# Two branch products as seven quarter products, gates through tanh, and places and order from tables in a hybrid decoder layer

## The chip, the cores and the metric

The kernel runs on one core of one Trainium2 chip. The metric is the device time of one execution in microseconds (us). Before the change it is 788.07 us, the median of three runs (787.36 to 788.13). Engines are called PE (TensorE, matrix products), ACT (ScalarE), DVE (VectorE), POOL (GpSimd) and SP (SyncE, which here issues transfers only); each runs its own instruction list in order and waits for the others by semaphores. POOL's list holds both its own arithmetic and the transfers that it issues.

## The reference

One decoder layer on a sequence of 512 tokens of width 1024, in float32. Three attention branches stand side by side: a sliding-window branch with sinks and bias (SWA), a stick-breaking branch (SB) and a cross attention to 256 memory tokens (MEM). Each has its own output product and a sigmoid gate; then come the output product, and a SwiGLU FFN of width 2816.

```python
u = rms_norm(h, ln_mix_pre[l])
proj = jnp.einsum('bsd,de->bse', u, w_in[l])
qa, ka, va, qb, kb, vb, qm, gl = jnp.split(proj, split_idx, axis=-1)
...
g = jax.nn.sigmoid(gl.reshape(B, S, N_BRANCH, D))
merged = (g[:, :, 0] * jnp.einsum('bse,ed->bsd', y_swa, w_branch_swa[l])
          + g[:, :, 1] * jnp.einsum('bse,ed->bsd', y_sb, w_branch_sb[l])
          + g[:, :, 2] * jnp.einsum('bse,ed->bsd', y_mem, w_branch_mem[l]))
mix = jnp.einsum('bsd,de->bse', merged, w_out[l])
h = h + rms_norm(mix, ln_mix_post[l])
...
ffn = jnp.einsum('bsf,fd->bsd', a, w_down[l])
h = h + rms_norm(ffn, ln_ffn_post[l])
```

Each branch output `y` is 512 x 512 and its product is 512 x 512 by 512 x 1024. The gate logits `gl` are 512 x 1024 by 1024 x 1024 for each branch.

## The kernel before, in words

**Products in three.** Every float32 operand is cut into a high part `hi` in a reduced format (an ACT copy, line 137) and the rest `lo` (a DVE subtraction, line 138). A product is the sum of three matmuls, hi x hi (line 169), hi x lo (170) and lo x hi (171). Nearly all have a left tile of 128 x 128 and 512 or 256 columns at the right.

**The stream of weights.** All products up to the gates run through one object, `Stream dn`. It is a list of units; a unit is one weight tile of up to 128 x 1024 that is loaded (tile `raw`, four buffers), split by ACT and DVE into `hi` and `lo` (four buffers each), and used by a generator of matmuls. Loads run four units ahead of the matmuls and splits three. The attention code calls `dn.run(us)` between its steps, which puts about so many microseconds of the stream's matmuls behind the step, so that PE has work while softmaxes and scans run on the other engines.

**Order of the stream.** Keys and queries of SB, values, keys of SWA, queries of SWA between the memory's keys and values, queries of MEM; then the branch product of SB, the gate of SB, the gate and the branch product of SWA, the gate and the branch product of MEM. Behind it come the transposes of the merged branches (`merge`) and the output product (`mx`).

**Gates as seven quarter products.** A gate product is cut into quarters of both operands and done as seven quarter products in place of eight (`QUART`, in the order p1, p2, p5, p3, p6, p7, p4), each in two weight units of 12 matmuls. The sums of weight quarters that this needs are made by transfers: `q_issue` adds a quarter from memory into a `raw` tile that is already there, on POOL's queue (line 446), six units ahead of its use. The sums of token quarters are made the same way from a second copy of the input, `xq` (lines 455 to 495), scaled on ACT. What a quarter product leaves in PSUM is kept by an ACT copy (line 540) or joined by DVE in `q_end`; p5 and p3 gather in one PSUM bank, and p1, p6, p7 and p4 in another.

**Branch products.** `branch_t` does a branch in the plain way: four token tiles, two column halves, four k steps. Its weight tiles come two a half, so a branch is four weight units. For SWA and MEM, DVE multiplies the PSUM result by the gate (line 599), and POOL adds what was there (line 602).

**Gates and tables of ACT.** `gated` applies Sigmoid on ACT. The softmaxes need Exp and the stick-breaking Ln and Exp, which lie in another table set than Sigmoid, so ACT loads tables several times (line 202 and others).

**What sets the order.** Each engine's list is in the order in which the program writes the instructions, with a scheduler and some explicit dependencies (`after`, `high_priority`, `later`) where it matters. PSUM is two pools, one of six banks (`aps`) and one of two (`dps`).

Of the kernel before, what the change touches and what calls it, by code (L numbers as in the profile page):

```python
# [17 lines left out]
P = 128  # L18
# [11 lines left out]
QM_FIRST = 3  # L30
WARM = 10

# [74 lines left out]
def tile_kernel(ctx, tc, a):  # L107
    nc = tc.nc
# [4 lines left out]
    psd = ctx.enter_context(tc.tile_pool(name="psd", bufs=2, space=bass.MemoryType.PSUM))  # L113
    psa = ctx.enter_context(tc.tile_pool(name="psa", bufs=6, space=bass.MemoryType.PSUM))
    drm = ctx.enter_context(tc.tile_pool(name="drm", bufs=1, space=bass.MemoryType.DRAM))

    first = ExitStack()
    wp = first.enter_context(tc.tile_pool(name="wp", bufs=4))
    cst = first.enter_context(tc.tile_pool(name="cst", bufs=1))

    def ck(name, dt=F32):
        return ckp.tile([P, 512], dt, tag="ck", name=name)

    def small(name, n=4):
        return sm.tile([P, 8], F32, tag="s", name=name)[:, :n]

    def dps(name):
        return psd.tile([P, 512], F32, tag="d", name=name)

    def aps(name):  # L130
        return psa.tile([P, 512], F32, tag="a", name=name)
# [14 lines left out]
    def w_load(src, n):  # L146
        uid[0] += 1
        raw = wp.tile([P, 1024], F32, tag="raw", name=f"raw{uid[0]}")
        nc.sync.dma_start(raw[:, :n], src)
        return raw  # L150

    def w_split(raw, n):
        uid[0] += 1
        hi = wp.tile([P, 1024], F32R, tag="hi", name=f"hi{uid[0]}", bufs=4)
        lo = wp.tile([P, 1024], F32R, tag="lo", name=f"lo{uid[0]}", bufs=4)
# [32 lines left out]
    def after(ins, first):  # L188
        dep = mybir.DependencyInfo(mybir.DependencyClass.NoSync, mybir.DependencyReason.DATA)
        tc.add_manual_dep(ins.ins, first.ins.name, dep, reason="order")  # L190

# [17 lines left out]
    def const(name, shape, pool=cst):  # L209
        t = pool.tile(shape, F32, name=f"c_{name}")  # L210
        nc.sync.dma_start(t[:, :], a[name])
        return t
# [3 lines left out]
    ones = cst.tile([P, P], F32, name="ones")  # L216
# [11 lines left out]
    def rstd_of(name, acc, n, bank):  # L228
# [6 lines left out]
        rb = cst.tile([P, n], F32, name=f"rb_{name}")  # L235
# [5 lines left out]
        rs = cst.tile([P, n // P], F32, name=f"rs_{name}")  # L241
# [46 lines left out]
    def proj(kind, idx):  # L288
        def gen(hi, lo):
            begun = first_ps.get((kind, idx))  # L290
            ps = begun or (aps if kind == "kb" or (kind, idx) == ("qb", 2) else dps)(f"{kind}{idx}")
# [6 lines left out]
            def evac():  # L298
                with tc.high_priority():
                    nc.vector.scalar_tensor_tensor(t[:, :], ps[:, :], s, st["rb"][:, :], op0=ALU.mult, op1=ALU.mult)  # L300
# [14 lines left out]

    def sigmoids(b):

        st.setdefault("sigmoid", set()).add(b)
        for f in st.pop(f"raw{b}", ()):
            f()  # L320

    def val(h, q):
        def gen(hi, lo):
            if q == 0:
                st["pv"] = [aps(f"pv{h}{t}") for t in range(NT)]
            for i in range(3 if q < 2 else 2):
                k = 3 * q + i
                for t in range(NT):
# [3 lines left out]
                    if k == KC - 1:  # L332
                        with tc.high_priority():
# [4 lines left out]
                                None,  # L338
                                op0=ALU.mult,
                            )  # L340
# [3 lines left out]
    v_all = cst.tile([P, NT * 640], F32, name="v_all")  # L344
# [32 lines left out]
    def mem_split():  # L377
# [13 lines left out]
        dn.later(5.0, lambda: st.update(zip(("mrs", "mrb"), rstd_of("m", acc, M, dps))))  # L391

    def mem_keys(i):
        def gen(hi, lo):
# [7 lines left out]
            with tc.high_priority():  # L402
                nc.vector.tensor_tensor(t, ps[:, :M], st["mrb"][:, :], op=ALU.mult)
# [5 lines left out]
    def mem_vals(q):  # L409
        def gen(hi, lo):  # L410
            if q == 0:
                st["pmv"] = [aps(f"pmv{t}") for t in range(2)]
            for i in range(2):
                k = 2 * q + i
                for t in range(2):
# [3 lines left out]
                    if k == KC - 1:  # L419
                        vt = ck(f"mv{t}")  # L420
                        with tc.high_priority():
                            nc.vector.tensor_scalar(
                                vt[:, :], st["pmv"][t][:, :], st["mrs"][:, t : t + 1], None, op0=ALU.mult
# [8 lines left out]
    QBANK = dict(p1="x", p6="x", p7="x", p4="x", p5="y", p3="y", p2="w")  # L432
# [4 lines left out]
    def q_issue(b, p, c):  # L437
# [8 lines left out]
        nc.gpsimd.dma_start(t[:, :], src, accum_op=ALU.add)  # L446
# [9 lines left out]
    def x_quarters(j, i):  # L456
        for c in range(2):
            t = quarter[(j, i, c)] = ck(f"xq{j}{i}{c}")
            nc.sync.dma_start(t[:, :], a["xq"][:, i, 4 * j + 2 * c : 4 * j + 2 * c + 2].rearrange("p k n -> p (k n)"))

    def x_gained(out, x, j, c, g):
        for k in range(2):
            sl, kk = slice(k * 256, (k + 1) * 256), 4 * j + 2 * c + k
            nc.scalar.activation(out[:, sl], x[:, sl], AF.Identity, scale=g[:, kk : kk + 1])

    def q_sum1(c):

        x_gained(quarter[(1, 1, c)], quarter[(1, 1, c)], 1, c, g_neg)
        x_gained(quarter[(0, 1, c)], quarter[(0, 1, c)], 0, c, g_pre)
        nc.gpsimd.dma_start(quarter[(1, 1, c)][:, :], quarter[(0, 1, c)][:, :], accum_op=ALU.add)  # L470
        quarter[("p5", c)] = quarter.pop((1, 1, c))

    def q_sum2():

        for c in range(2):
            t = quarter[("p6", c)] = ck(f"xq6{c}")
            x_gained(t, quarter[(0, 0, c)], 0, c, g_neg)
            nc.gpsimd.dma_start(t[:, :], quarter[("p5", c)][:, :], accum_op=ALU.add)

    def q_gain(j):  # L480
        for c in range(2):
            x_gained(quarter[(j, 0, c)], quarter[(j, 0, c)], j, c, g_pre)

    def q_sum3():

        for c in range(2):
            t = quarter[("p3", c)] = quarter.pop((1, 0, c))
            nc.gpsimd.dma_start(t[:, :], quarter[("p6", c)][:, :], accum_op=ALU.add)

    def q_sum4():  # L490

        for c in range(2):
            x = quarter.pop((0, 1, c))
            nc.scalar.mul(x[:, :], x[:, :], -1.0)
            t = quarter[("p7", c)] = quarter.pop((0, 0, c))
            nc.gpsimd.dma_start(t[:, :], x[:, :], accum_op=ALU.add)
# [21 lines left out]
    def gated(b, t, h, x):  # L518

        fn(x[:, :], x[:, :], AF.Sigmoid, scale=st["rs"][:, t : t + 1])  # L520
        if b == SB:
            acc = acc_t[(t, h)]
            nc.vector.tensor_tensor(acc[:, :], acc[:, :], x[:, :], op=ALU.mult)
        else:
            gate_t[(b, t, h)] = x

    def gate_there(b, t, h, x):
        if b != SB:
            gate_t[(b, t, h)] = x
        if b in st.get("sigmoid", ()):  # L530
            dn.later(2.0, lambda: gated(b, t, h, x))
        else:
            st.setdefault(f"raw{b}", []).append(lambda: gated(b, t, h, x))

    def q_end(b, p, i):
        ps = qbank[(QBANK[p], i)]
        if p in ("p1", "p5", "p6", "p7"):
            t = qkeep[(p, i)] = ck(f"gq{b}{p}{i}")

            st["chain"] = nc.scalar.copy(t[:, :], ps[:, :])  # L540
        if p == "p2":
            t = qkeep.pop(("p1", i))
            nc.vector.tensor_tensor(t[:, :], ps[:, :], t[:, :], op=ALU.add)
            gate_there(b, i, 0, t)
        elif p == "p6":
            t = qkeep.pop(("p6", i))
            nc.vector.tensor_tensor(t[:, :], qbank[("y", i)][:, :], t[:, :], op=ALU.subtract)
            gate_there(b, i, 1, t)
        elif p == "p7":
            t, x = qkeep.pop(("p5", i)), qkeep.pop(("p7", i))  # L550
            nc.vector.tensor_tensor(t[:, :], t[:, :], x[:, :], op=ALU.subtract)
            gate_there(b, 2 + i, 1, t)
        elif p == "p4":
            t = ck(f"gq{b}{p}{i}")
            fn(t[:, :], ps[:, :], AF.Sigmoid, scale=st["rs"][:, 2 + i : 3 + i])
            if b == SB:
                acc = acc_t[(2 + i, 0)]
                nc.vector.tensor_tensor(acc[:, :], acc[:, :], t[:, :], op=ALU.mult)
            else:
                gate_t[(b, 2 + i, 0)] = t  # L560

    def quart(b, p, c):
        def gen(hi, lo):
            for i in range(2):
                key = (QBANK[p], i)
                first = p in ("p1", "p5", "p2") and c == 0
                if first:
                    qbank[key] = (dps if p == "p2" else aps)(f"g{b}{p}{i}")
                for k in range(2):
                    mm3_behind(qbank[key][:, :], q_left(p, c, k, i), cols((hi, lo), k * 512, 512), first and k == 0, c == 1 and k == 1)  # L570
                yield 1.36
                if c == 1:
                    q_end(b, p, i)
# [3 lines left out]
    def branch_t(b, h, q):  # L577


        def gen(hi, lo):  # L580
# [3 lines left out]
            for t in range(NT):  # L584
# [7 lines left out]
                if b == SB:  # L592
                    acc_t[(t, h)] = ck(f"bs{t}{h}")
                    with tc.high_priority():
                        nc.vector.tensor_copy(acc_t[(t, h)][:, :], ps[:, :])
                    continue
                g = gate_t[(b, t, h)]
                with tc.high_priority():
                    nc.vector.tensor_tensor(g[:, :], ps[:, :], g[:, :], op=ALU.mult)
                eng = nc.vector if (b, t) == (MEM, NT - 1) else nc.gpsimd  # L600
                more = acc_t[(t, h)] if b == SWA else gate_t[(SWA, t, h)]
                eng.tensor_tensor(g[:, :], g[:, :], more[:, :], op=ALU.add)
# [1060 lines left out]
```

## Time and profile before

| what | before |
|---|---|
| median of three runs | 788.07 us |
| the profiled execution | 787.54 us |
| its span on the core | 785.7 us |
| granted clock of PE | 0.999 |
| DVE busy | 595.4 us |
| ACT busy | 469.3 us |
| POOL busy | 123.2 us |

The span is what the profile covers: from the first instruction to the last on the core. The execution's time has 1.84 us more around it. Shares of busy time are averages over parts of the kernel with different limits, so the views that follow go by stretches of the span. In a row of a timeline the first number is the start in us, the second the duration; what stands in brackets is idle time of that engine before it and who ended it.

### The profile page before, as it was taken

How to read it: one execution, taken by the hardware profiler on the slowest of the kernel's cores; microseconds unless marked ns; L12 is line 12 of the kernel's file. 1: busy time of each engine (PE TensorE's matmuls, PEld its weight loads, DVE VectorE, ACT ScalarE, POOL GpSimd, SP SyncE). 2: the span in 40 equal slices, each digit the busy share in tenths (PEclk: the TensorE clock that was granted, in tenths of full speed). 3: DMA queues.
4: the chain of work that ended last, by engine and by line, in shares of the span. 5: the costliest groups of instructions: out<-in, count | busy, mean ns of one | idle time of the engine just before them, and what ended most of it. 6: DMA issues, size and time to landing. Idle time of an engine off the chain costs nothing.

```text
span 785.7 us, 12335 instructions
## 1 busy us (share of the span) xinstructions
PE 776.3 (99%) x4638; PEld 682.2 (87%) x4638; DVE 595.4 (76%) x942; ACT 469.3 (60%) x837; POOL 123.2 (16%) x142
## 2 busy tenths in 40 slices
PE   9999999999999999999999999999999999999996
PEld 6899887788888888887888899999999999888885
DVE  6995876686877757876855599867677777898797
ACT  7663676686577666657633577455554455666673
POOL 0203400002011111321261000100000000215200
PEclk9999999999999999999999999999999999999999
DMA  8444923265449794369849418987666651949802
GB/s 301 132 138 121 314 88 108 81 190 124 89 100 206 178 208 139 54 170 250 304 162 255 92 47 219 260 220 191 186 180 183 186 155 54 222 107 239 184 1 108
DMA packets 44220, 128.61 MB, mean 164 GB/s; under 512 B 5248, under 2 KB 6832, under 8 KB 44160
## 3 DMA queue, kind: packets, MB, share of 16 engines
q1 hardware_dynamic: 30480, 85.21, 32.8%
q0 software_dynamic: 13248, 42.22, 27.8%
q8 instruction: 36, 0.59, 0.3%
q10 hardware_dynamic: 432, 0.39, 0.1%
q14 instruction: 24, 0.20, 0.1%
HBM read 120.98 MB, written 4.72 MB: 160 GB/s over the span
## 4 chain that ended last, share of the span: by engine, by line
PE 93%; DMA 2%; DVE 2%; issue 1%; ACT 1%; POOL 0%; DVEq 0%; SPq 0%; ACTq 0%; POOLq 0%
PE gx L169 5%; PE gx L171 5%; PE gx L170 5%; PE gy L171 3%; PE gy L169 3%; PE gy L170 3%; PE x L171 3%; PE x L170 3%; PE x L169 3%; PE br L169 2%; PE br L170 2%; PE br L171 2%; PE mx L171 2%; PE mx L170 2%; PE mx L169 2%; PE g1p L169 2%
## 5 line engine op out<-in xcount | busy, mean ns | idle before, releaser
L137 ACT CAST hi<-gw 128x1024 fp32r<-128x1024 f32 x77 | 79.9, 1048 | 92.7 <-DVE gw L1242 39.6
L138 DVE TENSOR_TENSOR lo<-raw,hi 128x1024 fp32r<-128x1024 f32 (+2 forms) x82 | 99.9, 1219 | 46.2 <-ACT hi L137 45.7
L138 DVE TENSOR_TENSOR lo<-gw,hi 128x1024 fp32r<-128x1024 f32 x77 | 93.5, 1223 | 36.2 <-ACT hi L137 36.2
L137 ACT CAST hi<-raw 128x1024 fp32r<-128x1024 f32 (+2 forms) x82 | 85.2, 1042 | 43.4 <-PE pv L171 13.0
L1224 POOL DMA_DIRECT2D gw<-in_w_gu x27 | 23.3, 883 | 196.4 <-DMA gw<-in_w_gu 91.3
L870 DVE TENSOR_TENSOR_SCAN bw<-br,bw 128x512 f32<-128x512 f32 (+3 forms) x32 | 24.4, 808 | 17.0 <-ACT bw L194 17.0
L137 ACT CAST hi<-r 128x1024 fp32r<-128x1024 f32 (+1 forms) x24 | 23.6, 982 | 19.8 <-PE y L171 5.3
L446 POOL DMA_DIRECT2D raw<-in_w_g x24 | 20.7, 862 | 93.2 <-DVE lo L138 74.2
L170 PE MATMUL x<-lo,lh 128*128 128x512 f32 x88 | 34.2, 389 | 0.0
L169 PE MATMUL x<-hi,lh 128*128 128x512 f32 x88 | 34.2, 389 | 0.0
L171 PE MATMUL x<-hi,ll 128*128 128x512 f32 x88 | 34.1, 389 | 0.0
L138 DVE TENSOR_TENSOR lo<-r,hi 128x1024 fp32r<-128x1024 f32 (+1 forms) x24 | 27.1, 1130 | 3.7 <-ACT hi L137 3.6
L137 ACT CAST hi<-bp 128x512 fp32r<-128x512 f32 x33 | 19.3, 620 | 13.4 <-PE y L171 4.8
L138 DVE TENSOR_TENSOR lo<-bp,hi 128x512 fp32r<-128x512 f32 x33 | 22.7, 721 | 6.0 <-ACT hi L137 5.8
L169 PE MATMUL gx<-B11h,hi 128*128 128x256 f32 x88 | 25.1, 285 | 0.2 <-ACT B11h L1153 0.2
L169 PE MATMUL gx<-T4h,hi 128*128 128x256 f32 x88 | 25.0, 285 | 0.0
L169 PE MATMUL gy<-N22h,hi 128*128 128x256 f32 x88 | 25.0, 284 | 0.0
L171 PE MATMUL gy<-N22h,lo 128*128 128x256 f32 x88 | 25.0, 284 | 0.0
L171 PE MATMUL gw<-B21h,lo 128*128 128x256 f32 x88 | 25.0, 284 | 0.0
L170 PE MATMUL gx<-B11l,hi 128*128 128x256 f32 x88 | 25.0, 284 | 0.0
L170 PE MATMUL gw<-B21l,hi 128*128 128x256 f32 x88 | 24.9, 283 | 0.0
L169 PE MATMUL gy<-T1h,hi 128*128 128x256 f32 x88 | 24.9, 283 | 0.0
(824 smaller groups left out, 2758.7 us busy)
## 6 DMA issues: line engine op xcount, KB each, us to landing
gw<-in_w_gu SPq DMA_DIRECT2D x57, 512.0 KB, 4.8
gw<-in_w_gu POOLq DMA_DIRECT2D x27, 512.0 KB, 7.5
raw<-in_w_g POOLq DMA_DIRECT2D x24, 512.0 KB, 6.0
raw<-in_w_g SPq DMA_DIRECT2D x18, 512.0 KB, 3.9
raw<-in_w_p SPq DMA_DIRECT2D x14, 512.0 KB, 4.5
raw<-in_w_brt SPq DMA_DIRECT2D x12, 512.0 KB, 4.8
bp<-in_w_dn SPq DMA_DIRECT2D x22, 256.0 KB, 10.3
r<-in_w_dn POOLq DMA_DIRECT2D x10, 512.0 KB, 9.1
```

Of the source, the lines that this page charges most:

```text
L137: ins = nc.scalar.copy(hi, raw)
L138: lows = nc.vector.tensor_tensor(lo, raw, hi.bitcast(F32), op=ALU.subtract)
L169: one = nc.tensor.matmul(out, lh, rh, start=start, stop=False, skip_group_check=True)
L170: nc.tensor.matmul(out, lh, rl, start=False, stop=False, skip_group_check=True)
L171: return one, nc.tensor.matmul(out, ll, rh, start=False, stop=stop, skip_group_check=True)
L446: nc.gpsimd.dma_start(t[:, :], src, accum_op=ALU.add)
L870: st["scan"] = nc.vector.tensor_tensor_scan(x, r, x, 0.0, op0=ALU.mult, op1=ALU.add)
L1224: nc.gpsimd.dma_start(gw[(n, key)][:, :], g_src(n, i, j), accum_op=ALU.add)
```

## The change

1. The branch products of SB and SWA are done as seven quarter products (`add_sevens`, `seven`), in the gates' manner: `seven_issue` adds weight quarters by transfers on POOL's queue, `seven_raw` copies the quarters of `y` on ACT and makes their four sums on POOL, `seven_split` splits these. A branch has seven weight units in place of four. MEM keeps `branch_t`.
2. Gates and branches share one way of joining quarter products (`group`, `ended`): an ACT copy for p1, p5, p6 and p7, a DVE operation where PSUM is read for p2, p3, p7 and p4, and POOL operations for the rest (`pooled`): two at p5, four at p6 and two at p7. PSUM banks come in turn from one list.
3. The gate is 0.5 (1 + tanh(0.5 x)): ACT does tanh and adds 1, the factor 0.5 stands in the values (`val`, `mem_vals`), and the multiplications and additions of SB and SWA go to POOL. For MEM, DVE does (g + 1) x product in one operation. One table set holds both Exp and Tanh.
4. Token quarters are rebuilt from `hi` and `lo` on POOL (`x_quarter`), and their sums are POOL operations (`x_sum`); the input `xq` and the ACT scaling go.
5. The stream's order changes (`EARLY`, `LATE`, memory loads at the values, SB's product ahead of SB's gate and SWA's ahead of SWA's gate); weight additions are issued seven units ahead in place of six. Attention steps are cut smaller, and some loads and copies move.
6. Tables in the source, made of numbers, fix the rest: `ORDER` gives each engine's instruction order, `PLAN` the place of each tile. All eight PSUM banks form one pool.

```diff
+EARLY = [("kb", 0), ("kb", 1), ("kb", 2), ("qb", 0), ("qb", 1)]
+LATE = [("qb", 2), ("kb", 3), ("qb", 3)]
+ORDER = {
+    "tensor": (
+        "0-196 198-235 197 236-363 385-405 364-384 406-408 430-441 450-457 409-429 442-449 458-475 480-481 483-485 "
...
+PLAN = {
+    "raw": (
+        "0 3 2 1 0 3 2 1 0 3 2 1 0 3 2 1 0 3 2 1 0 3 2 1 0 3 2 1 0 3 2 1 0 3 2 0 3 1 3 1 3 1 2 0 1 2 3 2 3 2 3 0 1 "
...
-    def gated(b, t, h, x):
-
-        fn(x[:, :], x[:, :], AF.Sigmoid, scale=st["rs"][:, t : t + 1])
-        if b == SB:
-            acc = acc_t[(t, h)]
-            nc.vector.tensor_tensor(acc[:, :], acc[:, :], x[:, :], op=ALU.mult)
...
+    def gated(b, t, h, g):
+
+        fn(g[:, :], g[:, :], AF.Tanh, scale=half_rs[:, t : t + 1])
+        if b == MEM:
+            gate_t[(b, t, h)] = g
+            return
+        nc.scalar.add(g[:, :], g[:, :], 1.0)
+        acc = acc_t[(b, t, h)]
+        nc.gpsimd.tensor_tensor(acc[:, :], acc[:, :], g[:, :], op=ALU.mult)
+        if b == SWA:
+            both = acc_t[(SB, t, h)]
+            nc.gpsimd.tensor_tensor(both[:, :], both[:, :], acc[:, :], op=ALU.add)
...
+    def x_quarter(j, i):
+
+        for c in range(2):
+            t = quarter[(j, i, c)] = ck(f"xq{j}{i}{c}")
+            for k in range(2):
+                h, l = cols(u[4 * j + 2 * c + k], i * 256, 256)
+                out = t[:, k * 256 : (k + 1) * 256]
+                nc.gpsimd.tensor_tensor(out, h.bitcast(F32), l.bitcast(F32), op=ALU.add)
...
+    def pooled(out, x, y_, op):
+        ins = nc.gpsimd.tensor_tensor(out[:, :], x[:, :], y_[:, :], op=op)
+        if "issued" in st:
+            after(ins, st["issued"])
+        return out
+
+    def ended(name, p, i, out):
+
+        ps = qbank[i]
+        if p == "p1":
+            qkeep[("p1", i)] = copied(f"{name}{p}{i}", ps)
+        elif p == "p2":
+            out(i, 0, joined(f"{name}2{i}", ps, qkeep[("p1", i)], ALU.add))
+        elif p == "p5":
+            x = qkeep[("p5", i)] = copied(f"{name}{p}{i}", ps)
+            one = qkeep.pop(("p1", i))
+            qkeep[("z", i)] = pooled(one, x, one, ALU.subtract)
+        elif p == "p3":
+            qkeep[("y", i)] = joined(f"{name}3{i}", ps, qkeep[("z", i)], ALU.add)
+        elif p == "p6":
+            x, z, c = copied(f"{name}{p}{i}", ps), qkeep[("z", i)], qkeep.pop(("y", i))
+            pooled(z, z, x, ALU.subtract)
+            out(i, 1, pooled(c, c, x, ALU.subtract))
+        elif p == "p7":
+            c = joined(f"{name}7{i}", qkeep.pop(("z", i)), ps, ALU.subtract)
+            pooled(qkeep[("p5", i)], qkeep[("p5", i)], c, ALU.subtract)
+            out(2 + i, 1, c)
+        else:
+            out(2 + i, 0, joined(f"{name}4{i}", ps, qkeep.pop(("p5", i)), ALU.add))
...
+    def seven_raw(b, c, ps):
+
+        for i in range(2):
+            if c % 2 == 0:
+                yq[(b, c // 2, i)] = ck(f"yq{b}{c // 2}{i}")
+            nc.scalar.copy(yq[(b, c // 2, i)][:, (c % 2) * 256 : (c % 2 + 1) * 256], ps[:, i * 256 : (i + 1) * 256])
...
+                nc.gpsimd.tensor_tensor(out[:, :], x[:, :], y_[:, :], op=op)
...
+    def seven(b, p):
+        def out(t, h, x):
+            acc_t[(b, t, h)] = x
+
+        def gen(hi, lo):
+            group(f"br{b}", p)
+            for i in range(2):
+                for k in range(2):
+                    mm3_behind(qbank[i][:, :], seven_left(b, p, k, i), cols((hi, lo), k * 512, 512), k == 0, k == 1)
+                yield 1.36
+                ended(f"br{b}", p, i, out)
...
     for b in (SB, SWA, MEM):
+        if b != MEM:
+            add_sevens(b)
...
-                    dn.units[g0 + 2 * g + c - 6]["begin"].append(lambda b=b, p=p, c=c: q_issue(b, p, c))
+                    dn.units[g0 + 2 * g + c - 7]["begin"].append(lambda b=b, p=p, c=c: q_issue(b, p, c))
...
-        if b != SB:
-            add_branch(b)
+    add_branch(MEM)
```

More of the change, by code (lines that the diff above doesn't have):

```diff
@@ L147, in w_load @@
         uid[0] += 1
-        raw = wp.tile([P, 1024], F32, tag="raw", name=f"raw{uid[0]}")
+        raw = places.take(wp, "raw", [P, 1024], F32, f"raw{uid[0]}")
         nc.sync.dma_start(raw[:, :n], src)
@@ new lines, in copied, with group @@
+    def copied(name, ps):
+        t = ck(name)
+        with tc.high_priority():
+            st["chain"] = nc.scalar.copy(t[:, :], ps[:, :])
+        return t
+    turns = [0]
+    def group(name, p):
+        turns[0] += 1
+        qbank.update({i: (dps if turns[0] % 2 else aps)(f"{name}{p}{i}") for i in range(2)})
+    def pooled(out, x, y_, op):
[3 more added lines that the diff above has]
+        return out
@@ L1040, in tile_kernel @@
             dn.run(us)
-    table("sigmoid_and_others")
-    sigmoids(SB)
-    sigmoids(SWA)
-    dn.until(f"gates{SWA}")
-    table("natural_log_exp_and_others")
+    dn.until(f"branch{SB}")
     for h in (0, 2):
@@ L1048, in tile_kernel @@
             dn.run(us)
-    table("sigmoid_and_others")
-    sigmoids(MEM)
+    dn.until(f"gates{SWA}")
     def bcast(name):
@@ L1219, in g_raw @@
         uid[0] += 1
[L1220 removed]
+        gw[(n, key)] = places.take(fp, "fraw", [P, 1024], F32, f"gw{uid[0]}")
         nc.sync.dma_start(gw[(n, key)][:, :], g_src(n, i, j))
@@ L1343, in tile_kernel @@
     gain_out = []
-    ssd = [small(f"ssd{t}", 2) for t in range(NT)]
+    ssd = Late(lambda t: small(f"ssd{t}", 2))
     held = []
@@ L1360, in dn_issue @@
             if p == "p1":
-                rr[c] = fp.tile([P, 1024], F32, tag="raw", name=f"r{c}")
+                rr[c] = places.take(fp, "fraw", [P, 1024], F32, f"r{c}")
                 nc.sync.dma_start(rr[c][:, :n], src)
@@ L1573, in tile_kernel @@
     go(len(fs.units))
+    for e, text in ORDER.items():
+        seen, last = getattr(nc, e).seen, None
+        for part in text.split():
+            a, _, b = part.partition("-")
+            for k in range(int(a), int(b or a) + 1):
+                if last is not None:
+                    follow(seen[k], seen[last])
+                last = k
 def _buckets():
```

518 lines of the change are left out of this document (320 added, 198 removed), and 105 rows, old and new, of tables (ORDER, PLAN).

## The prediction

> **What bounds the kernel now.** I read the page first, then the windows of 20 us over the attention and gate part, then the chain where it leaves PE, and last the timelines of VectorE (DVE) and GpSimd (POOL) side by side.
>
> ```profile
> PE 776.3 (99%) x4638; PEld 682.2 (87%) x4638; DVE 595.4 (76%) x942; ACT 469.3 (60%) x837; POOL 123.2 (16%) x142
> PE 93%; DMA 2%; DVE 2%; issue 1%; ACT 1%; POOL 0%; DVEq 0%; SPq 0%; ACTq 0%; POOLq 0%
> ```
>
> PE is busy for 776.3 of 785.7 us and is 93% of the chain. A removed matmul is therefore worth its full step, and any lateness of another engine that reaches PE is a loss of the same size. ACT (60%) has room. DVE (76%) has some, and the change gives most of its new work to POOL (16%).
>
> ```profile
> core 0: us, PE busy (x) PEld busy (x) DVE busy (x) ACT busy (x) POOL busy (x), PEclk, DMA share, GB/s
> 240.00:260.00 20.00, 20.00 (x90) 16.57 (x89) 15.73 (x22) 13.76 (x21) 3.38 (x4) 1.00 0.87 209
> 320.00:340.00 20.00, 20.00 (x109) 17.16 (x108) 17.65 (x31) 11.60 (x27) 6.50 (x6) 1.00 0.37 74
> 340.00:360.00 20.00, 19.03 (x84) 15.43 (x84) 12.17 (x13) 12.44 (x18) 5.63 (x7) 1.00 0.87 213
> 360.00:380.00 20.00, 19.53 (x87) 15.80 (x86) 15.75 (x19) 15.57 (x23) 0.84 (x1) 1.00 0.98 302
> sum 240.00, PE 238.56 PEld 197.99 DVE 170.32 ACT 146.25 POOL 53.46; mean PE 19.88 PEld 16.50 DVE 14.19 ACT 12.19 POOL 4.45
> ```
>
> The first row is a stretch of 512-column matmuls alone: some 88 begin in 20 us (two of the 90 only reach in), so one costs 0.227 us. The sum is over 180 to 420 us, the whole part that the change rewrites: PE is idle there for only 1.44 us, and DVE for 69.7. The idle is in two places, both before a token-half of the memory gate:
>
> ```profile
> 355.24 0.39 PE L171 MATMUL g2p<-hi,xsp51l 128*128 128x512 f32 x1
> 356.60 0.50 PE L169 MATMUL g2p<-hi,xsp30h 128*128 128x512 f32 x1 [0.97 <-ACT gq2p L540]
> 372.82 0.39 PE L171 MATMUL g2p<-hi,ul 128*128 128x512 f32 x1
> 373.68 0.50 PE L169 MATMUL g2p<-hi,uh 128*128 128x512 f32 x1 [0.47 <-ACT gq2p L540]
> 344.73 10.19 DMA raw<-in_w_g
> ```
>
> From start to start 1.36 and 0.86 us pass where 0.227 is due: 1.13 + 0.63 = 1.76 us lost. The ACT copy named is not the cause of the first: the chain goes back to a weight quarter that its queue adds together (10.19 us in flight).
>
> **What the change removes.** A plain branch product is 4 token tiles x 4 k x 2 column halves x 3 = 96 matmuls; seven quarter products need 7 x 2 x 2 x 3 = 84. For two branches 24 matmuls go, as the instruction lists of the two programs confirm (1953 to 1929 of 512 columns, the other PE shapes unchanged): 24 x 0.227 = 5.45 us off the bounding engine. This term is certain as long as PE sets the pace. The price is weight units of 1024 columns: seven a branch in place of four, so six more to load and split, and each now carries 12 matmuls, 2.7 us of PE, as the gates' units do.
>
> **What it adds, on engines beside PE.** The rows that price it:
>
> ```profile
> L602 POOL TENSOR_TENSOR gq0p<-gq0p,bs 128x512 f32<-128x512 f32 x8 | 10.7, 1332 | 40.1 <-DVE gq0p L599 40.1
> L602 POOL TENSOR_TENSOR gq2p<-gq2p,gq0p 128x512 f32<-128x512 f32 x6 | 8.1, 1343 | 32.1 <-DVE gq2p L599 30.8 <-issue 1.3
> L232 POOL TENSOR_TENSOR mT<-mT 128x256 f32<-128x256 f32 x1 | 0.7, 743 | 0.1
> L138 DVE TENSOR_TENSOR lo<-raw,hi 128x1024 fp32r<-128x1024 f32 x76 | 93.6, 1233 | 44.6 <-ACT hi L137 44.2 <-DMA wo<-in_w_out 0.3
> raw<-in_w_g POOLq DMA_DIRECT2D x24, 512.0 KB, 6.0
> L1058 POOL TENSOR_SCALAR bc_g_post<-bc_g_post 128x512 f32<-128x512 f32 x2 | 3.0, 1496 | 0.0
> L202 ACT ACT_TABLE_LOAD x8 | 10.3, 1283 | 0.1
> L540 ACT COPY gq0p<-g0p 128x512 f32<-128x512 f32 x8 | 4.7, 588 | 4.2 <-PE g0p L171 4.2
> ```
>
> ACT: 27 instructions more (copies of 256 to 1024 columns for 0.3 to 1.05 us) and three table loads less (3 x 1.283 = 3.8 us); tanh in place of Sigmoid is the same ACTIVATE form. Even at 27 x 1.05 = 28 us this lies under PE, with ACT idle for 240 - 146 = 94 us of the stretch. No table load is a releaser of PE, so their removal is worth nothing, and costs nothing should they return. DVE: 12 more, six splits of 1.23 and six of about 0.68, 11.5 us of its 69.7 idle. SP has ten DMAs less. The moved steps (attention in smaller pieces, loads two ahead, late copies) change what stands between a producer and PE. I find two spots where transposes follow their input at few matmuls' distance, the third stick-breaking head's scores and the last row block ahead of the FFN. By the waits of 1.13 and 0.63 us above they cost 0 to 3 us together; I take 1.2, as most of the moves give the producers more time, not less.
>
> POOL is the large term. Its TENSOR_TENSORs go from 18 to 106 (89 of 512 columns, 17 of 256): sums of token quarters, joins of the quarter products, gate multiplications. At 1.27 (start to start when back to back, just under the 1.28 of one) and 0.74 us that is 89 x 1.27 + 17 x 0.74 = 126 us, nearly all between 140 and 400 us. POOL alone has that time. The question is what DVE does meanwhile.
>
> **POOL and DVE hold each other up.** POOL's additions of before, and below them DVE's instructions around them:
>
> ```profile
> 309.21 1.29 POOL L602 TENSOR_TENSOR gq0p<-gq0p,bs 128x512 f32<-128x512 f32 x1 [24.28 <-DVE gq0p L599]
> 324.92 1.29 POOL L602 TENSOR_TENSOR gq0p<-gq0p,bs 128x512 f32<-128x512 f32 x1 [4.49 <-DVE gq0p L599]
> 329.32 1.58 POOL L602 TENSOR_TENSOR gq0p<-gq0p,bs 128x512 f32<-128x512 f32 x1
> 334.92 1.30 POOL L602 TENSOR_TENSOR gq0p<-gq0p,bs 128x512 f32<-128x512 f32 x1 [1.02 <-DVE gq0p L599]
> 340.12 1.29 POOL L602 TENSOR_TENSOR gq0p<-gq0p,bs 128x512 f32<-128x512 f32 x1 [3.90 <-DVE gq0p L599]
> 383.06 1.29 POOL L602 TENSOR_TENSOR gq2p<-gq2p,gq0p 128x512 f32<-128x512 f32 x1 [22.22 <-DVE gq2p L599]
> 386.25 1.60 POOL L602 TENSOR_TENSOR gq2p<-gq2p,gq0p 128x512 f32<-128x512 f32 x1 [1.91 <-DVE gq2p L599]
> ```
>
> ```profile
> 308.97 1.93 DVE L1006 TENSOR_SCALAR mw<-mw,mden 128x256 f32<-128x256 f32 x3
> 325.11 0.18 DVE L1003 RECIPROCAL mden<-mden 128x4 f32<-128x4 f32 x1 [0.27 <-ACT mw L194]
> 325.20 1.03 DVE L998 TENSOR_SCALAR mnm<-mnm 128x4 f32<-128x4 f32 x1
> 326.15 1.13 DVE L1006 TENSOR_SCALAR mw<-mw,mden 128x256 f32<-128x256 f32 x4
> 327.20 1.21 DVE L138 TENSOR_TENSOR lo<-raw,hi 128x1024 fp32r<-128x1024 f32 x1
> 329.13 2.72 DVE L1006 TENSOR_SCALAR mw<-mw,mden 128x256 f32<-128x256 f32 x4
> 334.77 0.67 DVE L138 TENSOR_TENSOR mpts31l<-mpt,mpts31h 128x512 fp32r<-128x512 f32 x1
> 340.44 2.06 DVE L138 TENSOR_TENSOR lo<-raw,hi 128x1024 fp32r<-128x1024 f32 x1 [0.40 <-ACT hi L137]
> 383.42 1.48 DVE L138 TENSOR_TENSOR wo14l<-wo,wo14h 128x512 fp32r<-128x512 f32 x1 [0.51 <-ACT wo14h L137]
> 386.03 0.68 DVE L138 TENSOR_TENSOR wo06l<-wo,wo06h 128x512 fp32r<-128x512 f32 x1
> 386.63 1.78 DVE L138 TENSOR_TENSOR wo07l<-wo,wo07h 128x512 fp32r<-128x512 f32 x1
> ```
>
> Four mw take 1.13 us alone and 2.72 beside POOL; a split of a weight takes 1.21 alone and 2.06; the 512-column splits 1.48 and 1.78 where 0.68 is usual. Each ends when POOL's addition ends. POOL is held as well: 1.58 and 1.60 us where it began inside a DVE instruction. The split of mpt, which lies in PSUM, is not held (0.67 at 334.77 beside 334.92). So a DVE instruction on SBUF data alone and a POOL TENSOR_TENSOR do not run together. Of L602's 14 additions six met such an instruction (those above but 334.92), for 1.08, 0.85, 1.59, 0.85, 0.80 and 1.10 us: 1.04 in the mean. None reached PE, because a weight is split up to three units ahead of its matmuls.
>
> [...]
>
> What it costs after, first as a floor. In the changed order the stretch from the SWA gate's first matmul to the memory branch's last holds 168 + 168 + 96 matmuls and 16 transposes of PE, 432 x 0.227 + 2 = 100 us. Its POOL queue has 41 TENSOR_TENSORs and four gain scalings (about 1.5 us), 58 us; its DVE queue 33 weight splits of 1.14 (step) and 17 SBUF-only operations of 0.60, 48 us: 106 us that exclude each other in 100. For the memory gate alone it is 20 x 1.27 + 14 x 1.14 + 9 x 0.60 = 47 in 38. A second such place is the end of the stick-breaking branch beside memory attention: 12 x 1.27 + 6 x 1.14 + 5 x 0.60 = 25 us in 20. The two are overfull by 6 + 5 = 11 us even if packed without a gap, and what comes late there is a weight split or a join that the mix waits for. The ceiling: 106 x 6/14 x 1.04 = 47 us of holds, all passed on to PE. DVE's idle, 58 us after the new work, can swallow holds only where the splits run ahead (three units of 12 matmuls, 8 us). I take the floor and a quarter of what lies between: 11 + 36/4 = 20 us, nearer to the floor since none of the six holds of before reached PE. Below nothing it can't go: an exclusion speeds nothing up. With POOL's queue full, its weight additions stand behind the two to four TENSOR_TENSORs of a join (2.5 to 5.1 us) though issued one unit earlier (2.7 us), so the 1.76 us are not won back in this case.
>
> **Sum**, against the profiled execution's 787.54 (span 785.7 and 1.84 around it): 787.54 - 5.45 + 20 = 802.1, and 0.53 more for the median of the runs, 788.07: 802.6, say 803.
>
> **Rivals.**
> - *The holds stay hidden.* For it: PE's idle of 1.44 us although six holds fell in that part, and three units of lead. Against: the overfull stretches. Time: 788.07 - 5.45 - 1.76 + 1.2 = 782.
> - *The queued weight additions come late*, the holds being harmless. A quarter sum is added into the tile of a quarter four units earlier: from that one's split to its own there are 4 x 2.7 = 10.9 us, of which 6.0 go in flight (the page's median for raw<-in_w_g on POOL's queue), so it decides once an issue stands more than 4.9 us behind that split. Three gates and two branches have 20 such quarters; if half come one TENSOR_TENSOR too late, PE loses 10 x 1.3 = 13 us: 788.07 - 5.45 + 13 = 796. For it: the one larger loss of before begins with such a weight. Against: it was 1.13 us.
> - *Even.* Contention costs just what the matmuls bring, 4 to 7 us: 788.
>
> **How the numbers follow.** Contention 0.53, late additions 0.06, hidden 0.33, even 0.08. Within 0.2% (1.6 us, about what a measurement can tell from no change) lies the even case alone: faster 0.33, same 0.08, slower 0.59. The likeliest's own range is 794 (floor) to 816 (two thirds of the way to the ceiling); to leave no more than 2 in 10 out the range takes in most of the hidden case: 781 to 816.
>
> **What would show it.** Right: PE's busy count down by 24 with idle of 10 us or more between 200 and 400 us, its releasers DVE splits (lo) or ACT copies behind them; DVE's 1024-column splits with a mean well over 1.23 us there; POOL TENSOR_TENSORs over 1.33. Late additions: DMA raw<-in_w_g as releaser on the chain, splits at 1.23. Wrong altogether: DVE splits unheld beside a full POOL, or held with PE still without idle; then the time is near 782.

## The result, and the profile after

The changed kernel takes 824.19 us (median of six runs, 820.45 to 825.98) against 788.05 for the kernel before: a ratio of 1.045, with a 95% interval of 1.0436 to 1.0466. That is slower, as forecast, but 8 us above the top of the range. The page of the profiled execution (825.98 us, span 824.2) has, against the rows shown of before:

```profile
PE 788.6 (96%) x4614; PEld 686.3 (83%) x4614; DVE 670.7 (81%) x954; ACT 481.0 (58%) x864; POOL 248.8 (30%) x230
PE 71%; DVE 8%; issue 7%; DMA 5%; POOL 4%; ACT 3%; SPq 0%; DVEq 0%; POOLq 0%; ACTq 0%
```

PE has 24 instructions less, as the change says (4638 to 4614), but its busy time went up by 12.3 us, from 776.3, and its idle time (span less busy) from 9.4 to 35.6. Its share of the chain fell from 93% to 71%. ACT rose by 12 us only; DVE rose by 75 with 12 instructions more. ACT loads tables six times in place of nine, for 1.28 us each: in the kernel before, loads at 303.45 and 328.22 us stand where ACT goes from the gate's Sigmoid to the memory softmax's Exp and back, here none stands between 137.10 and 423.03, where it does Exp and Tanh. (The stick-breaking does Sigmoid in both kernels, not Ln and Exp.) The waits of PE, longest first (total, times, longest), and DVE's largest group:

```profile
PE p L202 <- DVE lo L202: 12.1, 6, 5.3
PE p L202 <- DVE mpts20l L202: 3.5, 1, 3.5
PE p L202 <- DVE wide L202: 3.1, 2, 1.8
PE p L202 <- DVE br L202: 2.6, 1, 2.6
```

```profile
L202 DVE TENSOR_TENSOR lo<-raw,hi 128x1024 fp32r<-128x1024 f32 x126 | 195.6, 1560 | 39.7 <-ACT hi L202 39.3
```

(Nearly every instruction has line 202 here, that of the helper which records them; PSUM tiles are called p.) The splits of `raw` take 1.56 us in the mean where 1.23 was usual. One place shows why. The timeline of DVE, of POOL and of PE over the same microseconds of the memory gate:

```profile
362.54 0.68 DVE L202 TENSOR_TENSOR g<-p,g0p 128x512 f32<-128x512 f32 x1
363.25 7.82 DVE L202 TENSOR_TENSOR lo<-raw,hi 128x1024 fp32r<-128x1024 f32 x1
370.99 0.68 DVE L202 TENSOR_TENSOR g<-p,g0p 128x512 f32<-128x512 f32 x1
371.59 1.21 DVE L202 TENSOR_TENSOR lo<-raw,hi 128x1024 fp32r<-128x1024 f32 x1
```

```profile
362.92 0.87 POOL L202 DMA_DIRECT2D raw<-in_w_g  x1 [1.40 <-DVE lo L202]
363.52 1.58 POOL L202 TENSOR_TENSOR br<-br,g 128x512 f32<-128x512 f32 x1
364.78 1.56 POOL L202 TENSOR_TENSOR g0p<-g0p,g 128x512 f32<-128x512 f32 x1
366.03 2.73 POOL L202 TENSOR_TENSOR br<-br,g 128x512 f32<-128x512 f32 x2
368.47 1.51 POOL L202 TENSOR_TENSOR br<-br,br 128x512 f32<-128x512 f32 x1
```

```profile
365.46 0.39 PE L202 MATMUL p<-hi,uh 128*128 128x512 f32 x1
371.12 0.79 PE L202 MATMUL p<-lo,uh 128*128 128x512 f32 x1 [5.28 <-DVE lo L202]
371.72 0.63 PE L202 MATMUL p<-hi,ul 128*128 128x512 f32 x1
372.14 0.63 PE L202 MATMUL p<-hi,uh 128*128 128x512 f32 x1
372.57 0.63 PE L202 MATMUL p<-lo,uh 128*128 128x512 f32 x1
...
374.28 0.62 PE L202 MATMUL p<-hi,ul 128*128 128x512 f32 x1
374.70 0.44 PE L202 MATMUL p<-hi,uh 128*128 128x512 f32 x1
374.98 0.39 PE L202 MATMUL p<-lo,uh 128*128 128x512 f32 x1
```

A split that takes 1.21 us alone (371.59) takes 7.82, through five additions and multiplications that POOL has one after the other; PE waits for its low part for 5.28 us of idle. And then a second loss: the next matmuls start every 0.427 us (372.14, 372.57) in place of 0.227, until 374.7; below this is called half speed. Behind the first 6 us, where both kernels start at this step, 47 matmuls of 512 columns step at 0.427, in five runs, each behind a gap (from start to start, less 0.227): 7 behind 2.8 us at 241, 8 behind 1.8 and 1.4 at 262 and 264, 13 behind 3.6 at 293, 7 behind 5.4 at 365, 12 behind 1.2 and 3.8 at 388 and 392. A sixth run is of smaller matmuls, from 200.7 to 203.9 us behind a gap of 2.0 at 197, with a granted clock of 0.59 from 200 to 204.

The longest hold is another, just ahead of the gap at 241, through five of POOL's TENSOR_TENSORs as well:

```profile
234.61 8.45 DVE L202 TENSOR_TENSOR lo<-raw,hi 128x1024 fp32r<-128x1024 f32 x1
```

Behind it in DVE's queue stands a join (`br<-p,br1p`, 243.59), for which PE waits at 241.

By stretches (the columns are those of the windows above: PE, weight loads, DVE, ACT, POOL, then PE's granted clock, the share and the GB/s of DMA):

```profile
240.00:300.00 60.00, 51.01 (x227) 41.21 (x226) 55.62 (x76) 38.45 (x78) 28.29 (x23) 0.91 0.59 130
300.00:360.00 60.00, 60.00 (x258) 49.19 (x257) 45.54 (x38) 33.24 (x45) 41.35 (x34) 0.97 0.78 167
360.00:400.00 40.00, 28.42 (x107) 21.93 (x106) 37.51 (x20) 21.89 (x32) 24.95 (x22) 0.86 0.76 164
```

PE idles 9.0 us from 240 to 300, mostly beside the memory attention, nothing from 300 to 360, where POOL is busy for 41 us of 60, and 11.6 in the memory gate (360 to 400). Where PE idled, the granted clock is 0.91 and 0.86.

### The profile page after: what moved, and what is told of

Its sections match the earlier page's. It is cut to its first block, busy times and chain, and to the rows that moved or that the text cites. A ratio compares the mean times of both kernels' runs of the same rounds, so it can differ in the third digit from the quotient of the medians.

```text
span 824.2 us, 12412 instructions
## 1 busy us (share of the span) xinstructions
PE 788.6 (96%) x4614; PEld 686.3 (83%) x4614; DVE 670.7 (81%) x954; ACT 481.0 (58%) x864; POOL 248.8 (30%) x230
## 4 chain that ended last, share of the span: by engine, by line
PE 71%; DVE 8%; issue 7%; DMA 5%; POOL 4%; ACT 3%; SPq 0%; DVEq 0%; POOLq 0%; ACTq 0%
PE p L202 71%; DVE lo L202 3%; DMA raw<-in_w_g 2%; DMA wo<-in_w_out 2%; ACT hi L202 1%; POOL br L202 1%; POOL br1p L202 1%; DMA raw<-in_w_brt 1%; DMA xr<-in_x 1%; POOL g0p L202 1%; DVE s L202 1%; POOL g L202 1%; DVE w L202 1%; DMA mT<-in_memT 1%; POOL yq L202 0%
## 5 line engine op out<-in xcount | busy, mean ns | idle before, releaser
L202 DVE TENSOR_TENSOR lo<-raw,hi 128x1024 fp32r<-128x1024 f32 (+4 forms) x145 | 208.8, 1449 | 42.7 <-ACT hi L202 42.1
L202 ACT CAST hi<-raw 128x1024 fp32r<-128x1024 f32 (+4 forms) x145 | 143.6, 997 | 119.9 <-PE p L202 62.3
L202 ACT CAST hi<-wide 128x1024 fp32r<-128x1024 f32 x53 | 55.6, 1050 | 49.5 <-PE p L202 30.0
L202 DVE TENSOR_TENSOR lo<-wide,hi 128x1024 fp32r<-128x1024 f32 x53 | 65.6, 1239 | 22.6 <-ACT hi L202 22.6
L202 PE MATMUL p<-lo,uh 128*128 128x512 f32 (+1 forms) x160 | 58.6, 366 | 5.3 <-DVE lo L202 5.3
L202 PE MATMUL p<-hi,uh 128*128 128x512 f32 (+1 forms) x160 | 58.7, 367 | 4.4 <-DVE br L202 2.6
L202 PE MATMUL p<-lo,lh 128*128 128x512 f32 x154 | 59.9, 389 | 0.0
L202 PE MATMUL p<-hi,lh 128*128 128x512 f32 x154 | 59.9, 389 | 0.0
L202 PE MATMUL p<-hi,ll 128*128 128x512 f32 x154 | 59.7, 389 | 0.0
L202 PE MATMUL p<-hi,ul 128*128 128x512 f32 (+1 forms) x160 | 58.7, 367 | 0.0
```

What stands on the lines that cost most here:

```text
L202: ins = f(*args, **kw)
```

## The experiments

**POOL's operations without their reads.**

```diff
-        ins = nc.gpsimd.tensor_tensor(out[:, :], x[:, :], y_[:, :], op=op)
+        ins = nc.gpsimd.memset(out[:, :], 0.0)
```

and so at the six other places (the four additions of the memory's squares stay). The sums, joins and gate products are left out.

> The changed kernel with its 85 or so new POOL TENSOR_TENSORs each replaced by a MEMSET of the same output tile, which reads nothing in SBUF; all tables, queues and PE's work stay. Exclusion theory: DVE's splits of raw go back from 1.56 us in the mean to 1.23, PE's idle inside goes from 35 to under 10 us, its clock stays at 1.00, and the time is 779 to 788 us. Rival 'the tables' order makes the waits': 815 to 826, as the changed kernel. Rival 'late weight additions': 779 to 790 too, as POOL's queue gets shorter; the next run tells it apart.

785.55 us (ratio to before 0.997, 0.9961 to 0.9985). Page, DVE's group and the stretches:

```profile
PE 772.6 (99%) x4614; PEld 678.7 (87%) x4614; DVE 600.9 (77%) x954; ACT 480.9 (61%) x864; POOL 153.9 (20%) x230
```

```profile
L202 DVE TENSOR_TENSOR lo<-raw,hi 128x1024 fp32r<-128x1024 f32 x126 | 153.8, 1224 | 55.7 <-ACT hi L202 55.2
```

```profile
240.00:300.00 60.00, 60.00 (x294) 50.60 (x294) 47.57 (x70) 44.14 (x75) 19.78 (x34) 1.00 0.71 150
300.00:360.00 60.00, 60.00 (x266) 49.71 (x265) 36.73 (x41) 41.51 (x57) 24.83 (x41) 1.00 0.94 224
360.00:400.00 40.00, 40.00 (x186) 33.31 (x186) 29.57 (x39) 23.18 (x34) 15.95 (x21) 1.00 1.01 348
```

With all tables, queues and matmuls in place 38.6 us are gone. DVE's busy time falls by 69.8 us at the same instructions: that is how long it was held. Between the two profiled executions, which are 40.3 us apart, PE loses 24.3 us of idle (35.6 to 11.3; under 10 was expected) and 16.0 us of busy time, at a clock of 1.00. The tables' order is not what makes the waits.

**The same operations, shorter.**

```diff
-        ins = nc.gpsimd.tensor_tensor(out[:, :], x[:, :], y_[:, :], op=op)
+        ins = nc.gpsimd.tensor_tensor(out[:, :200], x[:, :200], y_[:, :200], op=op)
```

The other 312 columns of each are left out; the 16 sums of 256 columns stay whole.

> The changed kernel with its new 512-column POOL TENSOR_TENSORs working on 200 columns only (the rest of each tile is left as it is), so POOL's queue is as short as with the MEMSETs, but each still reads SBUF. Exclusion theory: the holds shrink with the POOL instruction from 1.28 to about 0.5 us, splits of raw at 1.30 to 1.40 us in the mean, time 788 to 805. Rival late weight additions: the same as the MEMSET run within 2 us. Rival order of the tables: 815 to 826.

788.74 us, splits at 1.30 us in the mean, DVE busy 616.7. At 0.39 of the width DVE is held for 15.8 us in place of 69.8, less than in proportion, and only 3 us more than with the MEMSETs reach the time: holds this short hardly reach PE.

**MEMSETs that keep POOL busy.** Three MEMSETs a place in place of one.

```diff
+        one, two, ins = (e.memset(out, 0.0) for _ in range(3))
```

> As the first run, but three MEMSETs in place of each new POOL TENSOR_TENSOR, about 1.6 us of POOL for 1.28, so POOL's queue is longer than in the changed kernel and still nothing in SBUF is read. Exclusion theory: splits of raw at 1.23 us, PE idle within 8 us of the first run's, 785 to 794. Rival late weight additions (POOL's queue length): 805 to 830.

794.51 us, splits at 1.22, DVE busy 603.3, just past the upper end. POOL is busy for 254.5 us, as in the changed kernel (248.8), and holds nothing, yet the time is 9.0 us above the first run: PE waits for 2.6 us at 376 us, and the chain goes back through MEMSETs on POOL to a weight addition (`raw<-in_w_g`) queued among them; twelve matmuls at half speed follow. So up to 9 of the 38.6 us belong to POOL's long queue, and about 30 to the holds.

**The same load on the kernel before.**

```diff
                 yield 1.36
+                nc.gpsimd.tensor_tensor(dum[:, :], dum[:, :], dum[:, :], op=ALU.add)
```

> The kernel before with 84 POOL TENSOR_TENSORs of 128x512 on a scratch tile added, one behind each 12 half-unit matmuls of the three gates; nothing waits for them. Exclusion theory: splits of raw in the gates go from 1.23 to 1.5 us or more, and PE is held where the split lead is used up: 792 to 815. Rival late weight additions: slower as well, by the same as the next run. Rival order: 788 within 2.

> As the run before, but with two MEMSETs of 128x512 in place of each added TENSOR_TENSOR (about 1.04 us of POOL for 1.28). Exclusion theory: splits at 1.23, time 787 to 790. Rival late weight additions: as slow as the run before.

844.58 and 806.87 us. Both lie outside their ranges. They came out at another place than meant: as nothing holds the added operations back, the scheduler put them ahead, into the first 130 us, where POOL was then nearly full (up to 19 of each 20 us). So the splits of the gates, which the expectation names, were not touched (1.24 us in the mean from 250 to 420); those of the first 140 us take 1.63. What remains is the comparison: 84 reading operations, 110 us of POOL, cost 38 us more than 168 MEMSETs of together 90 us, with PE idle for 53.5 us of the span, and the MEMSETs alone cost 19 by what they delay. As the two queues are not equally long, the pair does not tell how much of the 38 us the reads make; it speaks for a share of the queue's length too.

**All of them on DVE.** DVE's order table takes in POOL's instructions (g and their number) where their inputs are ready.

```diff
-        ins = nc.gpsimd.tensor_tensor(out[:, :], x[:, :], y_[:, :], op=op)
+        ins = on_dve(out[:, :], x[:, :], y_[:, :], op=op)
```

> The changed kernel with all 102 new TENSOR_TENSORs of POOL on DVE, each placed in DVE's order where its inputs are there; the result is the same and the other tables stay. DVE gets about 86 x 0.60 + 16 x 0.34 = 57 us of work, and loses every hold. Exclusion theory: splits of raw at 1.23, time 786 to 800 (what DVE's own queue now delays). Rival order of the tables: 815 or more. Rival DVE has no room: over 805 with splits at 1.23.

794.12 us, splits at 1.22: 30 us off with nothing left out, though DVE is busy for 53 us more than in the MEMSET run (653.9 against 600.9). What is left is DVE's queue: gaps of 2.0 us at 196 (attention) and 1.8 and 1.8 at 253 to 255 (memory attention), and 1.7 at 50.

**Half of them on DVE.** The joins and the sums of y's quarters in one run, the gate multiplications and additions in the other.

> The changed kernel with the 48 POOL operations of joins and of y's quarter sums on DVE, the other 58 (gate multiplications and additions, x quarters) left on POOL. Exclusion theory: each POOL TENSOR_TENSOR holds DVE for about 0.68 us (70 us of DVE's busy time over the MEMSET run, by 102), so holds fall to some 40 us and DVE gains 29 us of work: 797 to 812, between the changed kernel and the run with all of them on DVE. Rival that one group alone does it: 792 to 797 or over 818.

> The other part: the 30 gate multiplications and additions on DVE, joins, sums and x quarters (76) on POOL. Exclusion theory: 803 to 818. Rival that one group alone does it: 792 to 797 or over 818, opposite to the run before.

807.94 and 812.09 us. 48 operations moved bring 16.3 us, 30 bring 12.1; together 28.4 of the 30.1 of all 102. The 1.7 us left for the 24 sums of x's quarters, early in the kernel, are less than the 4 us between the two executions of each run, so they cost little. Per operation it is 0.34 and 0.40 us: no group is alone to blame.

**Without the tables.** `ORDER = {}`, and then `PLAN = {}` too.

> The changed kernel with the order tables emptied (the scheduler and the explicit dependencies order the instructions), the places kept. Same arithmetic, POOL's 106 TENSOR_TENSORs stay. Exclusion theory: still slow, 805 to 850, splits of raw over 1.4. Rival order of the tables: 785 to 797.

> As the run before, with the places' tables emptied too (pools hand out tiles). Exclusion theory: within 10 us of the run before. Rival places make the waits: 10 us or more faster than it.

853.0 and 859.26 us, the first 3 us above its range. The order tables are worth 29 us to the changed kernel, the places, without them, 6. The rival that the tables make the waits is out.

**A mixed version.** 81 operations on DVE, 25 on POOL, some placed later in DVE's order.

> 81 of the 106 POOL operations on DVE (the four sums of the memory's squares too), 25 left on POOL, among them the last additions of the memory branch and 15 of 16 x quarters; on DVE each stands where its inputs are there, some up to 15 us later so that DVE's attention operations are not behind them. The result is that of the reference. Exclusion theory: PE gaps at 49, 196 and 253 us of the run with all on DVE (1.7, 2.0 and 3.5 us) go or shrink, 784 to 790 us; under 787 it beats both kernels. Rival DVE has no room: 793 or more.

794.29 us, no better than all on DVE, and not in the range. The gaps at 49 and 196 us shrank or went, but one stayed. DVE, POOL and PE there:

```profile
248.94 1.23 DVE L209 TENSOR_TENSOR lo<-raw,hi 128x1024 fp32r<-128x1024 f32 x1 [0.17 <-ACT hi L209]
250.85 4.07 DVE L209 TENSOR_TENSOR lo<-raw,hi 128x1024 fp32r<-128x1024 f32 x1 [0.68 <-ACT hi L209]
254.84 0.68 DVE L209 TENSOR_TENSOR mpts00l<-p,mpts00h 128x512 fp32r<-128x512 f32 x1
```

```profile
251.03 2.80 POOL L209 TENSOR_TENSOR g1p<-g1p,g1p 128x512 f32<-128x512 f32 x2
```

```profile
251.35 0.50 PE L209 MATMUL p<-mpts00h,mvs0h 128*128 128x512 f32 x1 [0.91 <-ACT mpts00h L209]
255.57 0.79 PE L209 MATMUL p<-mpts00l,mvs0h 128*128 128x512 f32 x1 [3.72 <-DVE mpts00l L209]
```

Two joins, back to back, hold a split that PE doesn't need yet for 2.84 us; behind it in DVE's queue stands the split of `mpts`, which reads PSUM, and PE waits for that. Beside POOL such a split is not held: in the changed kernel four of them, from 264.64 to 267.11 us, take 0.67 to 0.68 us each beside two TENSOR_TENSORs of POOL (264.45 to 267.29).

**Two operations more.**

```diff
-337 343 339-342 350
+337 343 339-342 g89 g90 350
```

> The mixed version with only two more POOL operations on DVE: the two joins of the SB gate's p5, which in the mixed run stand back to back on POOL at 251.03 us (2.80 us) and hold a split from 1.22 to 4.07 us; they come behind the four mpts splits on DVE. Exclusion theory: that split takes 1.22, PE's gaps at 250 and 251 us (1.1 and 4.0) shrink to 2 us or less together, the nine matmuls at half speed behind them go (9 x 0.2 = 1.8), so 5 us off: 787 to 790. Rival DVE has no room: the gap stays at 3.5 us as with all on DVE, 792 or more.

789.91 us (ratio 1.0026, 1.0014 to 1.0038): 4.4 us off by moving two instructions. The split at 251.13 us takes 1.22, the gap of 4.0 is 1.2, and with the one of 1.0 before it 2.2, a little over what was expected; against the expectation seven matmuls at half speed still follow, though no gap there is longer than 1.2 us:

```profile
251.64 0.49 PE L209 MATMUL p<-mpts00h,mvs0h 128*128 128x512 f32 x1 [0.89 <-ACT mpts00h L209]
253.02 0.50 PE L209 MATMUL p<-mpts00l,mvs0h 128*128 128x512 f32 x1 [0.89 <-DVE mpts00l L209]
...
253.86 0.63 PE L209 MATMUL p<-mpts01l,mvs1h 128*128 128x512 f32 x1
254.28 0.63 PE L209 MATMUL p<-mpts01h,mvs1l 128*128 128x512 f32 x1
```

Of the versions that do the whole computation this is the fastest, and it does not beat the kernel before.

**Pauses of PE alone.** In the kernel before, in the SWA gate, eight times:

```diff
+        one = mm(ps[:, :P], dum[:, :P], dum[:, :P], True, True)
+        for _ in range(n):
+            nc.gpsimd.memset(dum[:, :], 0.0)
+        st["products"] = mm(ps[:, :P], dum[:, :P], dum[:, :P], True, True)
```

> The kernel before with eight pauses of PE put into the SWA gate, behind quarter products, each a chain of matmul, 1 to 6 MEMSETs of POOL (0.53 us each) and matmul: gaps of about 1, 1.5, 1.5, 2, 2, 2.5, 2.5 and 3.5 us. Pause theory (half speed follows a gap of some 2.5 us by itself): behind the three longest gaps some 8 matmuls of 512 columns start every 0.427 us, 1.6 us each, behind the shortest none, and the time is 788 plus the gaps (17) plus about 5: 806 to 813. Rival (half speed comes from what else runs in the changed kernel, as POOL's or DVE's load): all matmuls at 0.227, 803 to 806.

814.45 us, 1.5 above the range (the added matmuls were not counted in it). PE around the first pause with two MEMSETs and around the next longer one:

```profile
282.54 0.38 PE L181 MATMUL pause<-dum 128*128 128x128 f32 x2
284.21 0.49 PE L181 MATMUL pause<-dum 128*128 128x128 f32 x2 [1.29 <-POOL dum L443]
...
286.16 0.39 PE L170 MATMUL g0p<-lo,xsp30h 128*128 128x512 f32 x1
286.39 0.39 PE L171 MATMUL g0p<-hi,xsp30l 128*128 128x512 f32 x1
...
294.30 0.49 PE L181 MATMUL pause<-dum 128*128 128x128 f32 x2 [1.86 <-POOL dum L443]
...
295.67 0.63 PE L170 MATMUL g0p<-lo,xsp60h 128*128 128x512 f32 x1
296.10 0.63 PE L171 MATMUL g0p<-hi,xsp60l 128*128 128x512 f32 x1
...
298.23 0.63 PE L170 MATMUL g0p<-lo,xsp60h 128*128 128x512 f32 x1
298.65 0.48 PE L171 MATMUL g0p<-hi,xsp60l 128*128 128x512 f32 x1
```

Behind the three pauses of 1.3 to 1.45 us more than a matmul's step, and behind one of 1.6, all goes on at 0.23 us a matmul. Behind the two of 2.0 and the two of 2.6 follow 7, 8, 7 and 5 matmuls at 0.427. The pause of six MEMSETs came out at 1.6 us in place of 3.5, as matmuls of the memory attention were put into it. So a pause alone brings the slow matmuls, without the changed kernel's load on POOL and DVE, and about 2 us can do it, less than the expectation had. The slow matmuls behind the first of the longer pauses last for 3 us (295.67 to 298.65); in the changed kernel the run behind the gap at 293 lasts 5.5 us. What sets either length is not shown.

## Why the prediction was wrong

**Right: the side and the cause.** The changed kernel is slower mainly because POOL's TENSOR_TENSORs and DVE's operations on SBUF data exclude each other; with the reads gone, or with the operations on DVE, 38.6 and 30.1 of its us are gone. What the prediction named as proof came: splits far over 1.23 us, POOL's operations mostly at 1.5 to 1.8, PE idle behind DVE's lo. What it read from the trace of before is borne out as to who is held: DVE's splits of SBUF data (up to 8.45 us for 1.21) and POOL's operations (every 2.24 us for 1.25, below), but not DVE's splits of PSUM data (0.67 to 0.68 us beside POOL at 264.64).

**Wrong: the size of the contention, 20 us.** Measured against the MEMSET run it is 38.6, of which up to 9.0 may be the length of POOL's queue. Two steps failed.

*"The ceiling: 106 x 6/14 x 1.04 = 47 us of holds."* In the trace of before each of POOL's additions behind a gate stands alone, 1.3 to 1.6 us long, and none of the six holds read there is longer than 1.59 us. In the changed kernel POOL has several in a row, and a DVE instruction can wait through all of them: 2.84 us through two (mixed version), and 7.82 and 8.45 us for one of 1.21 through five. Against the same instructions of the MEMSET run the eight longest holds, 1.95 to 7.2 us each, make 32.7 of the 69.8 us. DVE was held for 0.68 us by each of 102 operations, where the step had 6/14 x 1.04 = 0.45. The prediction names such rows itself, "the two to four TENSOR_TENSORs of a join (2.5 to 5.1 us)", but puts only a weight addition behind them, not DVE.

Not every row holds DVE throughout. At the end of the SWA gate DVE's splits get in between, and it is POOL that is held, starting every 2.24 us in place of 1.25:

```profile
351.39 2.27 POOL L202 TENSOR_TENSOR g<-g,g0p 128x512 f32<-128x512 f32 x1
353.62 2.28 POOL L202 TENSOR_TENSOR g0p<-g0p,g0p 128x512 f32<-128x512 f32 x1
355.87 2.28 POOL L202 TENSOR_TENSOR g<-g,g0p 128x512 f32<-128x512 f32 x1
```

```profile
353.05 1.70 DVE L202 TENSOR_TENSOR lo<-raw,hi 128x1024 fp32r<-128x1024 f32 x1 [0.54 <-ACT hi L202]
355.40 1.59 DVE L202 TENSOR_TENSOR lo<-raw,hi 128x1024 fp32r<-128x1024 f32 x1 [0.65 <-ACT hi L202]
```

The eight longest holds, and that of the mixed version, all stand in rows right behind a transfer that POOL issues (the DMA_DIRECT2D at 362.92 above); in rows that begin on an idle POOL, as here, no split takes more than 2.3 us. No run moves these issues, so whether they are the cause stays open.

The share that reached PE was near what was taken: 24.3 us of idle of 69.8 is 35%, against 20 of 47, 43%; with 69.8 in its place the prediction's own rule gives 11 + 58.8/4 = 25.7 us. That this fits is partly luck, as some of the idle belongs to the queue's length and some lies where the floor had none.

*A term that was missing: what a stall costs beyond itself.* PE is busy for 16.0 us more than in the MEMSET run with the same matmuls. 47 matmuls at 0.427 us are 47 x 0.2 = 9.4 of it, the smaller matmuls behind the gap at 197 another 1.6; the rest was not itemised. The pauses show that a stall by itself can be the cause. The kernel before had two stalls of 1.13 and 0.63 us and does not show it: from 356.94 and 374.02 us on, the matmuls behind them step at 0.23 to 0.24.

A slip changes little: the 1.2 us taken for the moved steps do not stand in the sum, which would be 803.3 by its own terms.

**The places of the floor.** Both stretches called overfull are places of loss, but not by their sums. The memory gate, 47 us in 38 by the prediction's own count, shows 11.6 us of idle (360 to 400); the SWA gate, summed with it to an excess of 6, shows none. At the end of the stick-breaking branch (220 to 240, POOL busy for 18.7 us and DVE for 16.4 of 20) PE idles for 0.37 us only, but the hold of 8.45 us begins there, and PE waits for 2.6 us at 241. The other 6.3 us of the 9.0 from 240 to 300 lie in the stick-breaking gate beside the memory attention, which was not named. A sum over a stretch says little of where a queue runs dry.

**The 24 matmuls.** They are off: PE's busy time in the MEMSET run is 3.7 us under that of before. That is less than 5.45, and the hoped-for 782 of a kernel without holds was 785.55, since other gaps took the place of the two gone at 355 and 373 us. The two spots that the prediction priced at 0 to 3 us cost 0.5 (210) and 1.2 us (457); the largest gap, 2.1 us at 49, it did not name. There four POOL additions of the memory's squares hold DVE: in the changed kernel two subtractions into `kbs` take 2.82 us beside two of them (42.17), and 1.39 at 49.27 (moved off POOL, the gap is 0.9 in the last mixed version).

**The late weight additions.** Given 13 us and a chance of 0.06 as a rival of its own, this is a real part: 9.0 us with POOL's queue long and nothing held. How much of it there is within the changed kernel, where holds and queue lengthen each other, is not told apart.

## What to carry to other kernels

Work moved to an idle engine isn't free when its operations and the busy engine's do not run together: look in the trace for an instruction that takes longer beside the other engine's, and set the upper bound of a hold by the longest row of such operations without a gap, not by one of them. What stands behind a held instruction in its queue is late too, even if it could run: moving two operations of 106 brought 4.4 us. And a stall of the matrix engine of some 2 us can cost 1.4 to 1.6 us on top (7 or 8 matmuls of 0.2 us more each), and two of 1.0 and 1.2 us close together did as well, so stalls want a price of their own beside their length.

## What the runs showed of the hardware that was not expected

- A DVE instruction that waits for POOL can be held through a whole row of POOL's TENSOR_TENSORs (7.82 us for 1.21, through five), in the longest cases right behind a transfer that POOL issues; in a row that began on an idle POOL the two took turns, POOL every 2.24 us in place of 1.25.
- Matmuls of 512 columns step at 0.427 us in place of 0.227 behind pauses of 2.0 us and more, for 2.1 to 3.4 us (up to 5.5 in the changed kernel); not behind 1.6 and less in the run with pauses. In the changed kernel single gaps of 1.8 and 2.1 us (at 384 and 50 us) did not bring it, one of 2.0 (at 197) did, and gaps of 1.0 and 1.2 us close together did in the last mixed version, so the length of one gap does not decide alone.
- MEMSETs on POOL do not hold DVE: splits of 1.22 us beside 254.5 us of busy POOL.
